# Convolution with residual: weight load as 16 rows on SP's queue, and residual semaphores shared by three

## Chip, cores and metric

The kernel runs on one core of one Trainium2 chip. The metric is the device time of one execution in microseconds (us), taken as the median of several runs. In the profile, times are counted from the start of the span.

## What is computed

A 3 x 3 convolution with zero padding over 16 images of 64 channels and 64 x 64 pixels, to 64 output channels, plus a residual of the same shape as the output; everything is float32 in memory.

```python
def setup_inputs():
    batch, c_in, h, w, c_out, k = 16, 64, 64, 64, 64, 3
    # x: (batch, c_in, h, w), weight: (c_out, c_in, k, k), residual: (batch, c_out, h, w)

x_pad = np.pad(x, ((0, 0), (0, 0), (pad, pad), (pad, pad)), mode='constant')
for b in range(batch):
    for co in range(c_out):
        for ci in range(c_in):
            for kh in range(k):
                for kw in range(k):
                    output[b, co] += weight[co, ci, kh, kw] * x_pad[b, ci, kh:kh+h, kw:kw+w]
return (output + residual).astype(np.float32)
```

## The kernel before

Two images make a pair: 128 partitions (image and channel) of 4096 pixels, 2 MB. There are eight pairs (`NPAIR`), and for each one load of x, one load of the residual and one store of the result. The residual tiles `ro0` to `ro7` all stay in SBUF; DVE adds the convolution into them in place, and they are stored. The raw images go through three buffers `xr` (`NXR`), the packed bfloat16 images through four buffers `xp` (`NXP`), the sums through two halves of PSUM, `ps[0]` and `ps[1]`.

The work of the engines, each with its own hand-written order inside one critical section (L118):

- **SP** issues all large transfers from one queue, in this order: x pair 0 (moved by `to_the_front` ahead of the start barrier), residual 0, x 1, residual 1, x 2, residual 2, then for p = 3 to 7 x p and residual p. Each x load from p = 3 first waits on `s_half` until ACT has read the pair that used the buffer. After the loads come the stores of pairs 0 to 4 (`NEARLY` = 5), each behind a wait `s_add >= 2p + 3`. The stores of pairs 5 to 7 (L77, issued after the section) wait until all engines have finished it.
- **GpSimd** makes a 64 x 64 identity (L133 to L135) and zeroes the borders of `xp` and parts of `wl` (L145 to L148).
- **ACT** issues the weight load `wraw`, 64 rows of 2304 B (L151), on its own queue, and then, for each image, casts the even rows and the odd rows of pixels into the two halves of `xp` (L159, L163).
- **PE** waits for the identity (`s_id`) and the weights (`s_w`), transposes the nine 64 x 64 slices of the weights into PSUM (L195), and then, for each image, runs 24 matmuls (6 weight tiles with 4 chunks of 512 columns; L83 with a weight load, L84 without).
- **DVE** casts the transposed weights into the bfloat16 tile `wl` in six pieces (L172), then adds, for each image, the even and the odd rows of pixels (L182, two instructions). The first of the two raises `s_add`, so `s_add` counts images whose first half is added; the second hands the PSUM half back to PE by `s_bank`.

DVE waits for residual p on a semaphore of its own, `s_r[p]`, once for each pair.

Of the kernel before, what the change touches and what calls it, by code (L numbers as in the profile page):

```python
# [8 lines left out]
FP32 = mybir.dt.float32  # L9
# [6 lines left out]
def kernel(  # L16
# [7 lines left out]
    nc = tc.nc  # L24
# [7 lines left out]
    NPAIR = B // 2  # L32
# [3 lines left out]
    NXR = 3  # L36
# [3 lines left out]
    res_bc = residual.rearrange("b c h w -> (b c) (h w)")  # L40
    out_bc = out.rearrange("b c h w -> (b c) (h w)")
    x_bc = x.rearrange("b c h w -> (b c) (h w)")
    w_flat = weight.rearrange("co ci kh kw -> co (ci kh kw)")

    pool = ctx.enter_context(tc.tile_pool(name="pool", bufs=1))
    psum = ctx.enter_context(tc.tile_pool(name="psum", bufs=1, space=bass.MemoryType.PSUM))

    ident = pool.tile([64, 64], FP32)
    ro = [pool.tile([128, NPIX], FP32, name=f"ro{p}") for p in range(NPAIR)]
    xr = [nc.alloc_sbuf_tensor(f"xr{i}", [128, NPIX], FP32) for i in range(NXR)]  # L50

    xp = [pool.tile([128, J + 1, W], BF16, name=f"xp{i}") for i in range(NXP)]
    wraw = nc.alloc_sbuf_tensor("wraw", [64, 576], FP32)
    wl = pool.tile([128, 2, 3, 2, 64], BF16)
    ps = [psum.tile([128, NCHUNK, JC, W], FP32, name=f"ps{i}") for i in range(2)]

    sem = lambda name: tc.alloc_semaphore(name)
    s_w = sem("s_w")
    s_x = [sem(f"s_x{i}") for i in range(NXR)]
    s_r = [sem(f"s_r{p}") for p in range(NPAIR)]  # L60
    s_out = sem("s_out")
    s_id = sem("s_id")
    s_wt = sem("s_wt")
# [4 lines left out]
    s_add = sem("s_add")  # L68

    def load_x(p):  # L70
        return nc.sync.dma_start(out=xr[p % NXR][:, :], in_=x_bc[128 * p : 128 * p + 128, :]).then_inc(s_x[p % NXR], 16)

    def load_ro(p):
        nc.sync.dma_start(out=ro[p][:, :], in_=res_bc[128 * p : 128 * p + 128, :]).then_inc(s_r[p], 16)

    def store(p):
        return nc.sync.dma_start(out=out_bc[128 * p : 128 * p + 128, :], in_=ro[p][:, :])  # L77

    def matmul(out_, lhsT, rhs, start, stop, ldweights):

        e = nc.tensor
        if ldweights:
            return e.matmul(out=out_, lhsT=lhsT, rhs=rhs, start=start, stop=stop, skip_group_check=True)  # L83
        return e.add_instruction(  # L84
            mybir.InstMatmult(
                name=nc.get_next_instruction_name(),
                engine=PE,
                ins=[e.lower_ap(rhs), e.lower_ap(lhsT)],
                outs=[e.lower_ap(out_)],
                start_tensor_calc=start,  # L90
                stop_tensor_calc=stop,
                tile_size=(128, 128),
                tile_position=(0, 0),
                bass_skip_group_check=True,
                ldweights=False,
            )
        )

    def to_the_front(dma):

        def fixed(ap):
            t = ap.bass_ap.tensor.name
            return mybir.PhysicalAccessPattern(
                ap=ap.ap, offset=ap.bass_ap.offset, dtype=ap.dtype, memref=t, memsetref=t + "_set", bass_ap=ap.bass_ap
            )

        front = nc.main_func.blocks[0].instructions
        here = nc.cur_bb.bb.instructions  # L110
        ins = here.pop()
        assert ins.name == dma.ins.name
        at = next(
            i for i, e in enumerate(front) if e.engine == mybir.EngineType.SP and isinstance(e, mybir.InstDrain)
        )
        front.insert(at, copy.replace(ins, ins=[fixed(a) for a in ins.ins], outs=[fixed(a) for a in ins.outs]))

    with tc.tile_critical(no_gpsimd_drain=True):  # L118

        for p in range(NPAIR):  # L120
            if p >= NXR:

                nc.sync.wait_ge(s_half, 2 * (p - NXR) + 3)
            i = load_x(p)
            if p == 0:
                to_the_front(i)
            load_ro(p)
        for p in range(NEARLY):
            nc.sync.wait_ge(s_add, 2 * p + 3)
            store(p).then_inc(s_out, 16)  # L130


        nc.gpsimd.memset(ident[:, :], 0.0).then_inc(s_id, 1)  # L133
        nc.gpsimd.wait_ge(s_id, 1)
        nc.gpsimd.affine_select(  # L135
            out=ident[:, :],
            in_=ident[:, :],
            compare_op=mybir.AluOpType.not_equal,
            fill=1.0,
            base=0,  # L140
            pattern=[[-1, 64]],
            channel_multiplier=1,
        ).then_inc(s_id, 1)
        for t in xp:
            nc.gpsimd.memset(t[0:64, 0, :], 0.0).then_inc(s_id, 1)  # L145
            nc.gpsimd.memset(t[64:128, J, :], 0.0).then_inc(s_id, 1)  # L146
        nc.gpsimd.memset(wl[0:64, 0, :, 1, :], 0.0).then_inc(s_id, 1)  # L147
        nc.gpsimd.memset(wl[64:128, 1, :, 0, :], 0.0).then_inc(s_id, 1)  # L148


        nc.scalar.dma_start(out=wraw[:, :], in_=w_flat[:, :]).then_inc(s_w, 16)  # L151
        for n in range(B):
            p, im = divmod(n, 2)
            hp = slice(64 * im, 64 * im + 64)
            x4 = xr[p % NXR].rearrange("q (j two w) -> q j two w", two=2, w=W)
            t = xp[n % NXP]
            if im == 0:
                nc.scalar.wait_ge(s_x[p % NXR], 16 * (p // NXR + 1))
            i = nc.scalar.copy(out=t[64:128, 0:J, :], in_=x4[hp, :, 0, :])  # L159
            i.then_inc(s_half, 1)  # L160
            if n >= NXP:
                i._wait_ge(s_conv, n - NXP + 1)
            nc.scalar.copy(out=t[0:64, 1 : J + 1, :], in_=x4[hp, :, 1, :]).then_inc(s_pack, 1)  # L163


        nc.vector.wait_ge(s_wt, 1)
        tpf = ps[0].rearrange("p c j w -> p (c j) w")

        blocks = ((0, 0, 0, 0), (1, 0, 0, 1), (1, 0, 1, 0), (0, 1, 0, 2), (0, 1, 1, 1), (1, 1, 1, 2))
        for half, d, par, kh in blocks:  # L170
            hp = slice(64 * half, 64 * half + 64)
            i = nc.vector.tensor_copy(out=wl[hp, d, :, par, :], in_=tpf[0:64, 3 * kh : 3 * kh + 3, :])  # L172
        i.then_inc(s_bank, 2)
        for n in range(B):
            p, im = divmod(n, 2)
            hp = slice(64 * im, 64 * im + 64)
            o4 = ro[p].rearrange("q (j two w) -> q j two w", two=2, w=W)
            psj = ps[n % 2].rearrange("q c j w -> q (c j) w")
            if im == 0:
                nc.vector.wait_ge(s_r[p], 16)  # L180
            for par in range(2):
                i = nc.vector.tensor_tensor(  # L182
                    out=o4[hp, :, par, :], in0=psj[64 * par : 64 * par + 64, :, :], in1=o4[hp, :, par, :], op=ADD
                )
                if par == 0:
                    i._wait_ge(s_conv, n + 1)

                i.then_inc(s_add if par == 0 or n == B - 1 else s_bank, 1)


        nc.tensor.wait_ge(s_id, 4 + 2 * NXP)
        nc.tensor.wait_ge(s_w, 16)
        wraw3 = wraw.rearrange("p (ci t) -> p ci t", t=9)
        for t in range(9):
            i = nc.tensor.transpose(out=ps[0][0:64, t // 8, t % 8, :], in_=wraw3[:, :, t], identity=ident[:, :])  # L195
        i.then_inc(s_wt, 1)
        with nc.Fori(0, B // NXP, 1, engines=[PE]):
            for n in range(NXP):
                nc.tensor.wait_ge(s_bank, 1).then_inc(s_bank, -1)
                nc.tensor.wait_ge(s_pack, 1).then_inc(s_pack, -1)  # L200
                order = [(1, 0), (1, 1), (0, 0), (0, 1), (2, 0), (2, 1)]
                for i, (kw, d) in enumerate(order):
                    xlo, xhi = max(0, 1 - kw), min(W, W + 1 - kw)
                    for c in range(NCHUNK):
                        j0 = JC * c
                        m = matmul(
                            ps[n % 2][:, c, :, xlo:xhi],
                            wl[:, d, kw, :, :].rearrange("q r c -> q (r c)"),
                            xp[n][:, j0 + d : j0 + d + JC, xlo + kw - 1 : xhi + kw - 1],
                            i == 0,  # L210
                            i == len(order) - 1,
                            c == 0,
                        )
                m.then_inc(s_conv, 1)
# [36 lines left out]
```

## Time and profile before

| | |
|---|---|
| median of 8 runs | 124.32 us (124.07 to 124.86) |
| profiled execution | 124.3 us, span 122.2 us |
| PE, matmuls | 86.7 us busy (71%) |
| DVE | 75.2 us busy (61%) |
| ACT | 62.0 us busy (51%) |
| DMA | 50.48 MB, mean 413 GB/s |
| transposes of the weights, L195 | 9, 1.1 us busy |
| weight casts, L172 | 6, 1.9 us busy |
| weight load, issue to landing | 8.3 us |

The page splits the span into 40 slices of 3.06 us and gives for each the busy tenths of an engine, the mean busy share of the 16 DMA engines and the GB/s they moved. In the list of instructions, a line has start, length, engine, line of the code, operation, output and input, and in brackets the idle time before it with what ended it. In a view by windows, the columns after each engine's busy time are the granted clock of PE, the DMA share and GB/s. PE's clock is given as a share of full speed. "SPq" and "ACTq" are instructions that issue DMAs; q1 is SP's queue of DMA packets and q10 is ACT's.

### The profile page before, as it was taken

What the parts mean: (1) busy time and instruction counts of PE and PEld (TensorE: products, weight loads), DVE (VectorE), ACT (ScalarE), POOL (GpSimd) and SP (SyncE); (2) the same over time, 40 slices, a digit from 0 to 9 for tenths busy, and PEclk for the clock granted to TensorE, in tenths of its full rate; (3) what the DMA queues carried; (4) which work ended last, traced back from release to release, by engine and by line L of the source; (5) the groups of instructions that cost most, each with busy time, mean ns of one, the idle gap of its engine ahead of it and who ended that gap; (6) DMA issues with size and microseconds to landing.
All of it is one profiled execution on the core that took longest, in us unless ns stands there. A gap on an engine that the chain in (4) does not pass through costs nothing.

```text
span 122.2 us, 729 instructions
## 1 busy us (share of the span) xinstructions
PE 86.7 (71%) x389; PEld 10.4 (9%) x105; DVE 75.2 (61%) x38; ACT 62.0 (51%) x33; POOL 2.2 (2%) x16
## 2 busy tenths in 40 slices
PE   0003799999999999999999999999999930000000
PEld 0003000101011110111010101011110100000000
DVE  0005100989889898898989889898898988000000
ACT  4009948966984993992995797599000000000000
POOL 5100000000000000000000000000000000000000
PEclk9999999999999999999999999999999999555555
DMA  6999999999999999999999999999999999999992
GB/s 177 436 331 429 418 429 429 429 429 429 429 429 429 424 434 424 429 429 429 429 429 429 429 429 429 429 429 429 429 434 429 429 429 445 434 434 429 434 434 107
DMA packets 3536, 50.48 MB, mean 413 GB/s; under 512 B 400, under 2 KB 400, under 8 KB 464
## 3 DMA queue, kind: packets, MB, share of 16 engines
q1 hardware_dynamic: 3456, 50.33, 97.7%
q10 hardware_dynamic: 80, 0.15, 0.4%
HBM read 33.70 MB, written 16.78 MB: 413 GB/s over the span
## 4 chain that ended last, share of the span: by engine, by line
PE 70%; DVEq 2%; DVE 2%; issue 0%
PE ps L84 53%; PE ps L83 17%; DVEq L118 2%; DVE ro L182 2%
## 5 line engine op out<-in xcount | busy, mean ns | idle before, releaser
L182 DVE TENSOR_TENSOR ro<-ps,ro 64x2048 f32<-64x2048 f32 x32 | 73.2, 2289 | 17.7 <-PE ps L84 17.2
L84 PE MATMUL ps<-xp,wl 128*128 128x504 bf16 (+1 forms) x288 | 80.0, 388 | 0.2
L159 ACT CAST xp<-xr 64x2048 bf16<-64x2048 f32 x16 | 30.3, 1896 | 21.4 <-DMA xr<-in_x_dram 21.2
L83 PE MATMUL ps<-xp,wl 128*128 128x504 bf16 (+1 forms) x92 | 35.8, 389 | 2.5 <-PEq L200 2.5
L163 ACT CAST xp<-xr 64x2048 bf16<-64x2048 f32 x16 | 30.4, 1897 | 0.4
L83 PEld LDWEIGHTS ps<-xp,wl 128*128 128x128 bf16 x96 | 9.5, 99 | 77.9 <-issue 77.9
L172 DVE CAST wl<-ps 64x192 bf16<-64x192 f32 x6 | 1.9, 347 | 10.6 <-PE ps L195 10.6
L195 PE MATMUL ps<-ident,wraw 64*64 64x64 f32 x9 | 1.1, 309 | 9.4 <-DMA wraw<-in_weight_dram 9.4
L159 ACT ACT_TABLE_LOAD x1 | 1.3, 1283 | 1.5 <-SPq L118 1.5
L195 PEld LDWEIGHTS ps<-ident,wraw 64*64 64x64 f32 x9 | 0.9, 166 | 9.4 <-issue 9.4
L146 POOL MEMSET xp<- 64x64 bf16 x4 | 0.6, 147 | 0.2
L145 POOL MEMSET xp<- 64x64 bf16 x4 | 0.6, 145 | 0.2
L148 POOL MEMSET wl<- 64x192 bf16 x1 | 0.3, 253 | 0.1
L147 POOL MEMSET wl<- 64x192 bf16 x1 | 0.3, 252 | 0.1
L135 POOL TENSOR_SCALAR_AFFINE_SELECT ident<-ident 64x64 f32<-64x64 f32 x1 | 0.2, 233 | 0.2 <-POOL ident L133 0.2
L133 POOL MEMSET ident<- 64x64 f32 x1 | 0.1, 145 | 0.5 <-SPq L118 0.5
L235 POOL MEMSET const-bfloat16-1.0<- 128x1 bf16 x1 | 0.1, 112 | 0.0
L235 POOL MEMSET const-uint8-127<- 128x1 uint8 x1 | 0.1, 112 | 0.0
L235 POOL MEMSET const-float32-1.0<- 128x1 f32 x1 | 0.1, 109 | 0.0
L235 POOL MEMSET const-float32-0.0<- 128x1 f32 x1 | 0.1, 104 | 0.2 <-issue 0.2
## 6 DMA issues: line engine op xcount, KB each, us to landing
xr<-in_x_dram SPq DMA_DIRECT2D x8, 2048.0 KB, 17.6
ro<-in_residual_dram SPq DMA_DIRECT2D x8, 2048.0 KB, 22.1
out_dram<-ro SPq DMA_DIRECT2D x8, 2048.0 KB, 28.7
wraw<-in_weight_dram ACTq DMA_DIRECT2D x1, 144.0 KB, 8.3
```

The lines of the kernel that those rows point to most:

```text
L83: return e.matmul(out=out_, lhsT=lhsT, rhs=rhs, start=start, stop=stop, skip_group_check=True)
L84: return e.add_instruction(mybir.InstMatmult(name=nc.get_next_instruction_name(), engine=PE, ins=[e.lower_ap(rhs), e.lower_ap(lhsT)], outs ...
L118: with tc.tile_critical(no_gpsimd_drain=True):
L145: nc.gpsimd.memset(t[0:64, 0, :], 0.0).then_inc(s_id, 1)
L146: nc.gpsimd.memset(t[64:128, J, :], 0.0).then_inc(s_id, 1)
L147: nc.gpsimd.memset(wl[0:64, 0, :, 1, :], 0.0).then_inc(s_id, 1)
L159: i = nc.scalar.copy(out=t[64:128, 0:J, :], in_=x4[hp, :, 0, :])
L163: nc.scalar.copy(out=t[0:64, 1 : J + 1, :], in_=x4[hp, :, 1, :]).then_inc(s_pack, 1)
L172: i = nc.vector.tensor_copy(out=wl[hp, d, :, par, :], in_=tpf[0:64, 3 * kh : 3 * kh + 3, :])
L182: i = nc.vector.tensor_tensor(out=o4[hp, :, par, :], in0=psj[64 * par : 64 * par + 64, :, :], in1=o4[hp, :, par, :], op=ADD)
L195: i = nc.tensor.transpose(out=ps[0][0:64, t // 8, t % 8, :], in_=wraw3[:, :, t], identity=ident[:, :])
L235: nc = _bacc.Bacc("TRN2", target_bir_lowering=False, num_devices=1)
```

## The change

The weight load leaves ACT. It is issued by SP, behind the first image load and ahead of the first residual load, and it has 16 rows: partition q holds the four output channels 4q to 4q + 3, 9216 B in one piece. A slice for a transpose is now 16 output channels by 64 input channels, so there are 36 transposes in place of 9, each with 64 columns of weights and a 16 x 16 identity as the moving operand; their outputs are written 4 elements apart into the same places of PSUM. The casts into `wl` are the same. The residual loads share three semaphores instead of eight; SP waits, before it issues residual load p for p = 3 to 7, for the first add of image 2(p - 3), and DVE waits for 16, 32 or 48.

```diff
-    ident = pool.tile([64, 64], FP32)
+    ident = pool.tile([16, 16], FP32)
...
-    wraw = nc.alloc_sbuf_tensor("wraw", [64, 576], FP32)
+    wraw = nc.alloc_sbuf_tensor("wraw", [16, 4, 576], FP32)
...
-    s_r = [sem(f"s_r{p}") for p in range(NPAIR)]
+    s_r = [sem(f"s_r{i}") for i in range(NXR)]
...
-        nc.sync.dma_start(out=ro[p][:, :], in_=res_bc[128 * p : 128 * p + 128, :]).then_inc(s_r[p], 16)
+        nc.sync.dma_start(out=ro[p][:, :], in_=res_bc[128 * p : 128 * p + 128, :]).then_inc(s_r[p % NXR], 16)
...
             if p == 0:
                 to_the_front(i)
+                nc.sync.dma_start(out=wraw[:, :, :], in_=w_flat.rearrange("(q u) f -> q u f", u=4)).then_inc(s_w, 16)
+            if p >= NXR:
+
+                nc.sync.wait_ge(s_add, 2 * (p - NXR) + 1)
             load_ro(p)
...
-            pattern=[[-1, 64]],
+            pattern=[[-1, 16]],
...
-        nc.scalar.dma_start(out=wraw[:, :], in_=w_flat[:, :]).then_inc(s_w, 16)
...
-                nc.vector.wait_ge(s_r[p], 16)
+                nc.vector.wait_ge(s_r[p % NXR], 16 * (p // NXR + 1))
...
-        wraw3 = wraw.rearrange("p (ci t) -> p ci t", t=9)
+        wraw4 = wraw.rearrange("q u (ci t) -> q u t ci", t=9)
         for t in range(9):
-            i = nc.tensor.transpose(out=ps[0][0:64, t // 8, t % 8, :], in_=wraw3[:, :, t], identity=ident[:, :])
+            for u in range(4):
+                i = nc.tensor.transpose(
+                    out=ps[0].rearrange("p c j (q u) -> p (c j) u q", u=4)[0:64, t, u, :],
+                    in_=wraw4[:, u, t, :],
+                    identity=ident[:, :],
+                )
         i.then_inc(s_wt, 1)
```

## The prediction

> **What bounds the kernel now.** I read the page's slices first: they show which resource is full.
>
> ```profile
> DVE  0005100989889898898989889898898988000000
> ...
> DMA  6999999999999999999999999999999999999992
> GB/s 177 436 331 429 418 429 429 429 429 429 429 429 429 424 434 424 429 429 429 429 429 429 429 429 429 429 429 429 429 434 429 429 429 445 434 434 429 434 434 107
> ...
> q1 hardware_dynamic: 3456, 50.33, 97.7%
> q10 hardware_dynamic: 80, 0.15, 0.4%
> ```
>
> The DMA engines are full from the first slice to the last. 50.33 MB at 429 GB/s are 117.3 us of a span of 122.2, so the transfers set the time. One slice is low while the engines are fully busy: the third (6.1 to 9.2 us), 331 against 429 GB/s, a loss of 0.23 x 3.06 = 0.70 us. The chain of waits, which ends in PE and DVE, must be read with this: behind it come three stores that the queues would have reached hardly earlier. Next, stages of the start:
>
> ```profile
> 3.00:6.00 3.00, 0.00 (x0) 0.00 (x0) 0.00 (x0) 0.00 (x0) 0.60 (x3) 1.00 1.06 438
> 6.00:9.00 3.00, 0.00 (x0) 0.00 (x0) 0.00 (x0) 0.00 (x0) 0.00 (x0) 1.00 0.95 326
> 9.00:12.00 3.00, 1.14 (x9) 0.93 (x9) 1.39 (x5) 2.86 (x2) 0.00 (x0) 1.00 1.01 431
> ```
>
> The last number is GB/s. The trace's packet records say what runs in the slow stretch: the 64 weight packets of 2304 B (q10) start between 5.09 and 8.34 us, four on each of the 16 engines between its 16 KB packets. From about 6.0 to 8.9 us a 16 KB packet takes 740 to 830 ns; before and after, 611 to 619. Following each engine packet by packet, the excess over 611 ns per large packet is 0.94 to 1.15 us, about 0.97 on all 16: some 0.42 us are the weight packets themselves, some 0.6 the slowed large ones. So 147 KB, worth 0.34 us at full rate, cost 0.97.
>
> Then the start of the compute chain:
>
> ```profile
> 9.12 1.90 ACT L159 CAST xp<-xr 64x2048 bf16<-64x2048 f32 x1 [6.32 <-DMA xr<-in_x_dram]
> ...
> 9.40 1.14 PE L195 MATMUL ps<-ident,wraw 64*64 64x64 f32 x9 [9.40 <-DMA wraw<-in_weight_dram]
> 10.58 1.97 DVE L172 CAST wl<-ps 64x192 bf16<-64x192 f32 x6 [10.58 <-PE ps L195]
> 11.04 1.90 ACT L163 CAST xp<-xr 64x2048 bf16<-64x2048 f32 x1
> ...
> 13.08 0.58 PE L83 MATMUL ps<-xp,wl 128*128 128x512 bf16 x1 [2.54 <-PEq L200]
> ```
>
> The image lands at 9.09 (records of landings), the weights at 9.27. Two branches meet at PE's first convolution, 13.08: ACT's casts end at 12.94, DVE's weight casts at 12.55. The image branch is last; the weight branch has 0.4 us to spare. From there PE runs without a gap (24 matmuls of 216 ns = 5.18 us an image) and DVE follows. The end:
>
> ```profile
> 98.90 4.61 DVE L182 TENSOR_TENSOR ro<-ps,ro 64x2048 f32<-64x2048 f32 x2 [0.58 <-PE ps L84]
> 103.81 1.76 SPq L77 DMA_DIRECT2D out_dram<-ro  x3
> ```
>
> The last three stores are issued from 103.81, 14.6 us of transfer. In the packet records their first packets start at 105.4 to 106.2, directly behind those of the fifth store, with no gap over 6 ns. The first DMA of the kernel, issued at 0.00, had its first packets at 1.01, so these could have started at 104.8. The two engines that land last began at 105.87 and 106.16: the compute chain has a slack of about **1.1 us** against the transfers (1.07 to 1.35). This decides everything below: a gain of the chain is worth nothing, a loss over 1.1 us shows in full.
>
> **What the Trainium skill says.** "DMA: Bandwidth & Descriptors", section "Queues, rings and completion order": each DMA engine takes turns between the queue rows that have work, packet by packet. The trace agrees: weight packets lie singly between large ones. "SBUF — State Buffer", "Door 1: The DMA port swizzle": partitions 0 to 63 reach 8 of 16 ports, 0 to 15 only 4, measured there at 104 GB/s. The trace has no 16-partition load; its 64-partition load does run in a stretch in which everything is 20% slower, which fits. "TensorE: Matmul & The Clock Gate", "LDWEIGHTS": a weight load takes its columns divided by 1.2 GHz, whatever the rows, and may run under the matmul before it; "Part 1" of that page: PE runs at half clock until a free-running window of 3.4 us was busy. The trace agrees with the last: matmuls are 427 ns apart until about 18.5, then 216.
>
> **The change, part by part.**
>
> *Weights on SP's queue.* They leave the second queue, so no packets alternate; on each engine one packet of 9216 B follows the eighth packet of the image and precedes the first residual. It is an issue of 0.33 us (the row of L74) ahead of seven loads on SP; the image load alone keeps the engines in work to about 7 us, so the delay to 1.33 is hidden. ACT loses an issue of 0.53 us while it waits for the image: nothing.
>
> Cost on the stream: at the rate of the large packets 9216/16384 x 611 = 344 ns. Ceiling: if four engines each share one of 4 ports, 147456 B / 104 GB/s = 1.42 us (an estimate with the page's figure). But the end is set by the engine that is last. From the records, without weight packets fifteen engines would finish the image at 6.5 to 7.1 us and the last at 7.59, since its first packet took 2.04 us. It comes to its port when the three others are 0.6 us into theirs: all four finish at about 8.35, a cost of 0.77 for the late one, and the other engines (6.95 + 1.4) are no later than it. So for the end: cost 0.34 to 0.77, against 0.97 now: a gain of 0.2 to 0.63. A loss is not excluded if the ports share badly. I take **-0.4 us**.
>
> *When image and weights land.* The last engine's image packets end at 7.59 instead of 8.34: it lands at about 8.3. The weights follow at 8.6 (no sharing) to 9.0 (ports); I take 8.8 against 9.27.
>
> *36 transposes for 9.* Now 107 ns apart (9 in 1.14 us, the tail included). Each new one has the same 64 columns of weights but 16 moving columns for 64. If the moving side sets the pace, it falls to a quarter, and the load of 64 columns, 53 ns by the page, sets it: 36 x 53 = 1.9 us. If the pace doesn't fall: 36 x 107 = 3.85. In the trace the second weight load ends 59 ns after the first, under the first matmul, so I take 65 ns: 2.3 us. Chain: 8.8 + 0.13 to start + 2.3 + 0.29 tail and signal + 1.97 casts + 0.2 to the matmul = **13.7**, against 13.08. The image branch (8.3 + 3.85) is ready at 12.2, so the weights are now last. PE, DVE and the last stores' issue move by +0.6; the slack of 1.1, less the 0.4 gained by the stream, covers 0.7. On the path: 0, barely. The clock adds noise: PE was at half clock for 5.4 us, and by the page's window it could be 3.4 to 6.8, which moves the chain by -1.0 to +0.7 us.
>
> *Residual semaphores by threes; a wait on s_add ahead of residual loads 3 to 7.* The SP queue stops there: behind it stand the next image load, then stores. Load p waits for the first add of image 2(p-3): 21.1 + 2.3 = 23.4 us for p = 3, then every 10.4 us, to 64.9 for p = 7; today they issue at 21.1 and every 9.8, to 60.4. With +0.6 that is up to 5.1 us later. The next image loads wait until 30.6, 40.4, 50.2 and 60.0 anyway, later than each add (24.0, 34.4, 44.8, 55.1), so none moves. The cover: the queued image load before the last residual lands at 77.6, 12 us after 65.5. Cost 0; were a gap to open, each us would cost one. The stores wait for s_add 3 to 11 as before, the last at 75.7, far ahead of their packets (101). DVE's waits see the same landings.
>
> *Identity 16 x 16*: on GpSimd, done by 3.7 us, under the image load.
>
> **Sum**: the profiled execution took 124.3 (span 122.2 + 2.1 around it), equal to the median 124.32. 124.3 - 0.4 = **123.9 us**. About 0.2% (0.25 us) is what a measurement tells from no change.
>
> **Rivals.**
> - *No gain on the stream.* The 20% stretch is a port or memory limit that stays with the bytes, or isn't the weights' doing: 16 rows into 4 ports cost 0.9 to 1.2 us like now. For: the slowdown begins on all engines at one moment, 6.0, not after each one's own weight packet, which speaks for something shared. Against: the late engine absorbs part. **124.3** (124.1 to 124.5).
> - *The transposes become the bound (slower).* Place: between the weights' landing and the first convolution. At 107 ns each: 8.8 + 0.13 + 3.75 + 0.29 + 1.97 + 0.2 = 15.1, +2.1 us; minus the slack of 1.1: +1.0, hence **125.3**, with an idle gap in the DMA near 104. It decides from +1.1 us, that is from about 80 ns a transpose. For: 107 ns is all that the trace shows for a pair; against: the 59 ns of the second load.
> - *The change doesn't do what it says*, the rows being split or ordered otherwise: as the first rival. The instruction order shows one 16-row load behind the first image, so this is small.
>
> **Chances.** Forecast 0.48 (123.6 to 124.15), no gain 0.29 (the split-row case included), transposes 0.23 (124.5 to 125.4, as the pace lies between). Most of the forecast is below 124.07: faster 0.45, same 0.30, slower 0.25. The range 123.6 to 125.1 leaves out the slowest end of the last and gains over 0.7 us, together under 2 in 10.
>
> **What would show it.** The third slice back above 400 GB/s, weight packets in q1, no 16 KB packet over 700 ns between 6 and 9 us: the stream step right. Weight packets of over 1 us: the ports. The transposes' busy time (about 2.4 us, or near 4) and the start of the first convolution (13.7 or over 14.5) decide the chain; a gap in the GB/s windows at 104 to 107 would show that its slack was used up. Residual loads issued up to 5 us later with no dip in GB/s show the waits free. I am wrong if the third slice recovers and the end doesn't follow, or if the image lands no earlier than 9 us.

## The result and the profile after

The changed kernel takes **125.33 us** (median of 11 runs, 124.57 to 126.09) against 124.28 (32 runs, 124.06 to 124.86) on the same chip: a ratio of 1.008, with a 95% interval of 1.0062 to 1.0098. It is slower by about 1.0 us, outside the predicted range.

The page of the changed kernel, its slices of the span, queues and transposes:

```profile
DVE  0000600689898898989889898898988989100000
...
DMA  7999999999999999999999999999999999999992
GB/s 182 422 272 427 427 427 433 427 433 427 427 427 427 427 427 427 427 427 427 427 427 433 427 427 427 433 427 433 427 433 427 427 427 443 433 427 433 427 449 117
...
q1 hardware_dynamic: 3488, 50.48, 98.2%
...
L199 PE MATMUL ps<-ident,wraw 16*64 16x16 f32 x36 | 2.3, 213 | 9.9 <-DMA wraw<-in_weight_dram 9.9
```

The weights are in q1 now, as intended, and the third slice has become worse: 272 GB/s where it was 331 and should have been over 400. The windows of the same trace (columns as before: busy times, clock, DMA share, GB/s):

```profile
3.00:6.00 3.00, 0.00 (x0) 0.00 (x0) 0.00 (x0) 0.00 (x0) 0.51 (x3) 1.00 1.00 426
6.00:9.00 3.00, 0.00 (x0) 0.00 (x0) 0.00 (x0) 0.11 (x1) 0.00 (x0) 1.00 1.05 279
9.00:12.00 3.00, 2.08 (x36) 2.11 (x36) 0.00 (x0) 2.98 (x2) 0.00 (x0) 1.00 0.94 399
```

From 6 to 9 us the DMA engines are fully busy (1.05) although the rate is low: the packets take longer, the engines don't wait. In the packet records, the 16 weight packets of 9216 B take 347 to 1099 ns, two of them over 1 us, and 17 of the 16 KB packets beside and behind them take 970 to 1570 ns, where 611 is usual. Weight packets and slowed large packets together come to 1.56 us an engine (1.03 in the kernel before, counted the same way). No engine is spared: the first of the 16 to land residual 0 does so at 13.42 us, 12.81 before. The start of the compute chain and its end, from the timeline:

```profile
8.89 1.90 ACT L162 CAST xp<-xr 64x2048 bf16<-64x2048 f32 x1 [6.65 <-DMA xr<-in_x_dram]
...
9.92 2.27 PE L199 MATMUL ps<-ident,wraw 16*64 16x16 f32 x36 [9.92 <-DMA wraw<-in_weight_dram]
...
12.22 1.97 DVE L175 CAST wl<-ps 64x192 bf16<-64x192 f32 x6 [12.22 <-PE ps L199]
...
14.49 0.58 PE L83 MATMUL ps<-xp,wl 128*128 128x512 bf16 x1 [2.30 <-PEq L208]
...
105.14 1.76 SPq L77 DMA_DIRECT2D out_dram<-ro  x3
```

The first convolution starts at 14.49 (13.08 before), the last stores are issued at 105.14 (103.81), 1.33 us later. But the windows from 103 to 112 us show no dip: 426, 431 and 426 GB/s. In the packet records these stores start at 106.16 at the earliest. Five engines have finished the store ahead by then and wait up to 0.4 us; the last one finishes it at 106.88 and goes on without a gap, so the end is not moved by this. The last landing is at 121.80 (121.28).

The span of this execution is 122.73 us, its time 125.94: **3.2 us lie outside the span**, where the kernel before has 2.1 (2.05 to 2.15 in all its executions whose spans are on record). Over 13 executions of the changed kernel, spans are 122.3 to 123.5 (mean 122.78; 122.09 in those executions of the kernel before), the time outside 2.03 to 3.29 (mean 2.47). So the loss has two parts: +0.7 in the span and +0.4 outside it. The prediction had no cause for the second at all.

### The profile page after: what moved, and what is told of

The parts are those of the page before. It is cut to its first block, busy times and chain, and to the rows that moved or that the text cites. A ratio compares the mean times of both kernels' runs of the same rounds, so it can differ in the third digit from the quotient of the medians.

```text
span 122.7 us, 779 instructions
## 1 busy us (share of the span) xinstructions
PE 87.6 (71%) x412; PEld 11.7 (10%) x132; DVE 75.2 (61%) x38; ACT 62.0 (50%) x33; POOL 2.1 (2%) x16
## 4 chain that ended last, share of the span: by engine, by line
PE 70%; DVEq 2%; DVE 2%; issue 0%
PE ps L84 53%; PE ps L83 17%; DVEq L118 2%; DVE ro L185 2%
## 5 line engine op out<-in xcount | busy, mean ns | idle before, releaser
L199 PE MATMUL ps<-ident,wraw 16*64 16x16 f32 x36 | 2.3, 213 | 9.9 <-DMA wraw<-in_weight_dram 9.9
L199 PEld LDWEIGHTS ps<-ident,wraw 16*64 16x64 f32 x36 | 2.2, 149 | 9.9 <-issue 9.9
```

The lines of the kernel that those rows point to most:

```text
L199: i = nc.tensor.transpose(out=ps[0].rearrange("p c j (q u) -> p (c j) u q", u=4)[0:64, t, u, :], in_=wraw4[:, u, t, :], identity=ident[:, :],)
```

## The experiments

Ratios are to the kernel before on the same chip, with 95% intervals. To compare streams, I take from the trace when residual 0, the first transfer behind the weights, lands: the mean over its 16 DMA engines (before 13.34 us, changed kernel 13.90).

**The place in the queue alone.** The 64 rows of before, moved to SP's queue behind the first image:

```diff
                 to_the_front(i)
+                nc.sync.dma_start(out=wraw[:, :], in_=w_flat[:, :]).then_inc(s_w, 16)
...
-        nc.scalar.dma_start(out=wraw[:, :], in_=w_flat[:, :]).then_inc(s_w, 16)
```

> The kernel before, with its 64 weight rows of 2304 B moved to SP's queue behind the first image load (nothing else changed). Theory (ports: the 16 rows share 4 SBUF ports, so each engine pays 1.5 us for them): 64 rows reach 8 ports, so the stall is about half, 0.7 us an engine against 0.97 of before; weights land near 9.0, chain unmoved; 124.0 to 124.2. Rival A (the place in SP's queue is what hurts, since an engine can't pass a slow weight packet): as slow as the change, 125.0 to 125.4. Rival B (only the transposes matter): 124.2 to 124.3.

Measured: 124.11 us, ratio 0.9998 (0.9991 to 1.0006). The third slice rises to 382 GB/s, residual 0 lands at 13.15, the first convolution starts at 12.14. The move does no harm, and hardly any good.

**The 16 rows alone**, on ACT's queue, with the 36 transposes and eight residual semaphores:

```diff
-        nc.scalar.dma_start(out=wraw[:, :], in_=w_flat[:, :]).then_inc(s_w, 16)
+        nc.scalar.dma_start(out=wraw[:, :, :], in_=w_flat.rearrange("(q u) f -> q u f", u=4)).then_inc(s_w, 16)
...
```

> 16 rows of 9216 B and 36 transposes, but issued on ACT's own queue, with the residual semaphores of before. Theory (ports): the same stall as in the change, large packets of over 1 us near the weight packets, last landing +0.5 us, chain +1.0 to +1.4: 124.9 to 125.4. Rival A (place in SP's queue): no stall on the stream; only the 36 transposes, chain +1.3: 124.5. Rival B (transposes alone): as the change, 125.3, with a stream like before.

Measured: 125.86 us, 1.0118 (1.0099 to 1.0136); third slice 278 GB/s, residual 0 at 14.22, time outside the span 2.50 to 2.94. That is slower than expected. Both parts of the loss are here without the queue being touched: they come with the 16 rows and what is built on them.

**The residual semaphores and SP's waits alone** (the diff's lines on `s_r` and `s_add`, nothing else):

> The kernel before with the residual semaphores by threes and the waits on s_add only. Theory and both rivals: 124.3, residual loads issued 3 to 5 us later and no change in GB/s. If the waits cost: over 124.6.

Measured: 124.16 us, 0.9999 (0.9988 to 1.0009). And the change without this part (16 rows on SP, eight semaphores, no wait on `s_add`):

> The change without its residual part: own semaphores for each pair, no waits on s_add ahead of residual loads. All theories: as the change, 125.0 to 125.5, span 122.3 to 123.3, with time minus span over 2.3 in some runs (PE's program is as long as in the change). Under 124.6 would say that the waits are part of the loss.

Measured: 125.38 us, 1.0089 (1.0056 to 1.0121), as slow as the whole change. The waits cost nothing in either direction.

**More transposes** in the kernel before, three small ones ahead of each of the nine:

```diff
         for t in range(9):
+            for u in range(3):
+                nc.tensor.transpose(out=ps[1][0:64, t // 8, t % 8, 16 * u : 16 * u + 16], in_=wraw3[0:16, :, t], identity=ident[0:16, 0:16])
```

> The kernel before with 27 more small transposes (16 rows, 64 columns of weights, 16 moving columns) whose output is not used; weight load as before. They add 27 x 59 ns = 1.6 us, of which 0.4 is spare: chain +1.2, stream as before. Theory (slack of 1.1 us at the end): 124.3 to 124.7, with more spread than before. Rival B (transposes are the whole loss): 125.2 or more.

Measured: 125.73 us, 1.011 (1.009 to 1.013). The 36 took 4.9 us, not the 2.3 of the changed kernel: 16-row transposes in a row start 59 ns apart, but a 64-row one starts 145 ns after a 16-row one, and a 16-row one 247 ns after a 64-row one. As a copy of the change's PE work this run failed. It measures something else well. Its last stores are issued at 107.67, 3.86 us later than before, and its windows show what the changed kernel's don't:

```profile
102.00:104.00 2.00, 0.73 (x4) 0.00 (x0) 1.42 (x2) 0.00 (x0) 0.00 (x0) 1.00 1.01 434
104.00:107.00 3.00, 0.00 (x0) 0.00 (x0) 2.97 (x2) 0.00 (x0) 0.00 (x0) 1.00 0.54 229
107.00:108.50 1.50, 0.00 (x0) 0.00 (x0) 0.38 (x1) 0.00 (x0) 0.00 (x0) 0.80 0.03 11
108.50:111.00 2.50, 0.00 (x0) 0.00 (x0) 0.00 (x0) 0.00 (x0) 0.00 (x0) 0.50 0.99 413
```

The transfers run dry (11 GB/s) until the stores come. This execution took 126.81 against 124.30, so 3.86 us of delay cost 2.51: the slack of the chain is about 1.3 us. The 1.33 of the changed kernel fit in, all the more as its stream is 0.5 us late itself.

**The load's form alone.** The 16 rows go behind the first image into a tile of their own, and the nine transposes work on a constant tile, so that PE's program is that of before. This version and the next three leave the weights out of the result.

```diff
+    wd = nc.alloc_sbuf_tensor("wd", [16, 2304], FP32)
...
+                nc.sync.dma_start(out=wd[:, :], in_=w_flat.rearrange("(q u) f -> q (u f)", u=4)).then_inc(s_w, 16)
...
+        nc.gpsimd.memset(wraw[:, :], 0.1).then_inc(s_id, 1)
...
-        nc.scalar.dma_start(out=wraw[:, :], in_=w_flat[:, :]).then_inc(s_w, 16)
```

> The 16-row load on SP's queue behind the first image load into a tile of its own, with PE's nine transposes of before reading a constant 64-row tile once that load has landed: the weights are left out of the computation, every instruction of the conv stays. So the load alone, without the 27 more transposes. Theory (ports): stall of 1.5 us an engine as in the change, weights landing near 9.8, first conv near 13.5, last landing +0.5 us, span 122.6, time minus span 2.07: 124.7. Rival B (transposes): 124.2.

Measured: 124.57 us, 1.0039 (1.0027 to 1.0051), 2.10 to 2.15 outside the span. The load's form costs 0.48 us, all inside the span. The same bytes as 128 rows of 1152 B, over all partitions:

> As the run before it, but the load is one of 128 rows of 1152 B over all 128 partitions (weights left out of the computation again). Theory (ports): each engine writes to a port of its own, no large packet over 640 ns, excess about 0.4 us an engine, image landing near 8.0: 123.8 to 124.1. If the stall comes from small packets or from the weights' place in memory: excess 0.7 or more, above the 64 rows of before.

Measured: 123.13 us, **0.9926** (0.9912 to 0.9941). The line of the window from 6 to 9 us, for the 16 rows and for the 128:

```profile
6.00:9.00 3.00, 0.00 (x0) 0.00 (x0) 0.00 (x0) 0.50 (x1) 0.00 (x0) 1.00 1.01 289
```

```profile
6.00:9.00 3.00, 0.77 (x8) 0.80 (x9) 0.00 (x0) 1.25 (x1) 0.00 (x0) 1.00 0.99 415
```

289 against 415 GB/s for the same bytes in the same place of the same queue. With 128 rows no large packet takes over 611 ns between 5.5 and 10 us. It is faster than expected: residual 0 lands 0.75 us earlier than before, and at the end the last engine is 0.3 us behind the median instead of 0.6. Is it the number of rows or that of the partitions' ports? 32 rows in partitions 0 to 31:

> The same with 32 rows of 4608 B in partitions 0 to 31, two packets an engine, eight ports (weights left out of the computation again). Theory (ports): as the 64 rows on SP's queue, excess about 0.7 us an engine, since the ports are the same eight: 124.0 to 124.2. If the size or number of packets decides: between 0.8 and 1.5 us.

Measured: 124.27 us, 1.0006 (0.9991 to 1.0022), third slice 354. And the 16 rows of 9216 B again, now in every eighth partition, which changes nothing but the partitions:

```diff
-    wd = nc.alloc_sbuf_tensor("wd", [16, 2304], FP32)
+    wd = nc.alloc_sbuf_tensor("wd", [128, 2304], FP32)
...
-                nc.sync.dma_start(out=wd[:, :], in_=w_flat.rearrange("(q u) f -> q (u f)", u=4)).then_inc(s_w, 16)
+                nc.sync.dma_start(out=wd[0:128:8, :], in_=w_flat.rearrange("(q u) f -> q (u f)", u=4)).then_inc(s_w, 16)
```

> The run with 16 rows of 9216 B and nine transposes on a constant tile (weights left out of the computation) again, with one thing changed: the rows lie in every eighth partition of 128, which reach 8 ports and not 4. Theory (ports): excess 0.7 to 0.9 us an engine against 1.3, last landing 0.4 us earlier, 124.1 to 124.3. If the size of the packets or their number decides: 124.6 and excess 1.3 as with adjacent rows.

Measured: 124.19 us, 0.9996 (0.9986 to 1.0006). The line of the window that had 289 GB/s above:

```profile
6.00:9.00 3.00, 0.00 (x0) 0.00 (x0) 0.00 (x0) 0.57 (x1) 0.00 (x0) 1.00 0.96 333
```

16 packets of 9216 B spread over the partitions cost what 32 or 64 smaller ones cost in the first 32 or 64, and 0.5 us less, by the ratios, than the same 16 in partitions 0 to 15. It is where the rows lie that counts. The Trainium skill ("SBUF — State Buffer", "Door 1: The DMA port swizzle") counts 4 ports for partitions 0 to 15, 8 for 0 to 31, for 0 to 63 and, by its formula, for every eighth, and 16 for all. It doesn't say what such a load does to other transfers. The runs fall into these three classes, and two pairs of them differ in the partitions alone as far as the load goes (the first and third row, the fourth and fifth):

| load of the weights | ports by the page | residual 0 lands | ratio |
|---|---|---|---|
| 16 rows in 0 to 15 | 4 | 13.72 | 1.0039 |
| 32 rows in 0 to 31 | 8 | 13.26 | 1.0006 |
| 16 rows in every eighth | 8 | 13.32 | 0.9996 |
| 64 rows in 0 to 63, SP's queue | 8 | 13.15 | 0.9998 |
| 64 rows in every second | 16 | 12.67 | 0.9944 |
| 128 rows | 16 | 12.59 | 0.9926 |

**A version that is faster.** The fifth row of the table computes everything: 64 rows of 2304 B in every second partition of a zeroed tile of 128, on SP's queue behind the first image, and nine transposes with a 128 x 128 permutation that brings the odd rows, all zero, out of the way.

```diff
-    wraw = nc.alloc_sbuf_tensor("wraw", [64, 576], FP32)
+    wraw = nc.alloc_sbuf_tensor("wraw", [128, 576], FP32)
...
+                nc.sync.wait_ge(s_z, 1)
+                nc.sync.dma_start(out=wraw[0:128:2, :], in_=w_flat[:, :]).then_inc(s_w, 16)
...
+        nc.gpsimd.memset(wraw[:, :], 0.0).then_inc(s_z, 1)
...
-            i = nc.tensor.transpose(out=ps[0][0:64, t // 8, t % 8, :], in_=wraw3[:, :, t], identity=ident[:, :])
+            i = nc.tensor.transpose(out=tpw[0:64, 128 * t : 128 * t + 128], in_=wraw3[:, :, t], identity=ident[:, :])
```

> A version meant to keep what the ports give: the kernel before, with its 64 rows of 2304 B on SP's queue behind the first image load, but in every second partition of 128, so that they reach 16 ports; GpSimd zeroes the tile first, SP waits for that, and the nine transposes take 128 rows and a 128 x 128 permutation. PE's program is as long as before. Theory (ports): excess about 0.45 us an engine, image landing near 7.9, weights near 8.2, transposes 9 x 213 ns, first conv near 12.5, last landing near 120.2: 123.2 to 123.5. If the ports are not the cause: as the 64 contiguous rows on SP's queue, 124.1.

Measured: 123.5 us, **0.9944** (0.9928 to 0.9960): faster than both kernels. Its page shows the third slice repaired:

```profile
GB/s 167 426 421 432 432 432 432 432 426 426 432 421 432 426 432 432 432 432 432 432 426 432 432 421 432 426 426 426 432 432 432 432 432 432 432 432 432 432 432 130
```

**The time outside the span.** In the traces of the changed kernel, of the 16 rows on ACT's queue and of the change without its residual part, the packet records hold one packet of 16 KB of a queue q8, kind "instruction", 1.7 to 2.4 us after the last instruction; the kernel before has none. In these three the packet ends 3.43, 3.17 and 2.80 us after the last instruction, and the time outside the span is 3.21, 2.93 and 2.58 us: 0.2 us less each time, so the one goes with the other. What these three share is PE's program, 54 instructions longer (27 more transposes, a weight load and a matmul each). So: the kernel before, with 27 transposes of the identity ahead of PE's wait for the weights, done while the image loads.

```diff
+        for t in range(27):
+            nc.tensor.transpose(out=ps[1][0:64, t // 8, t % 8, :], in_=ident[:, :], identity=ident[:, :])
         nc.tensor.wait_ge(s_w, 16)
```

> The kernel before with 27 transposes of the identity (54 more PE instructions, as many as the change adds) put ahead of PE's wait for the weights, where PE idles under the image load; their output is not used. Weight load, stream and chain as before. Theory T3 (in the change, PE's longer program costs 0.4 to 1.2 us outside the span in some runs, since more instructions have to be fetched): span 122.1 as before, time minus span above 2.1 in some runs, median 124.3 to 125.2. Rival (that time comes from something else in the change): time minus span 2.07 in every run, 124.2.

Measured: 124.55 us, 1.0036 (1.0016 to 1.0055), and not evenly: of 22 executions, 10 are like before (spans to 122.3, 2.0 outside), 5 have 2.46 to 3.58 outside, 7 have spans of 122.7 to 123.2. With nine such transposes in place of 27:

> As the run with 27 hidden transposes, with 9 of them (18 more PE instructions instead of 54). If the length of PE's program makes the time outside the span: fewer runs over 2.3 us, or none, median 124.1 to 124.3. If any hidden PE work does: as many as with 27 (5 of 22).

Measured: 124.10 us, 0.9992 (0.9983 to 1.0002); all as before. So hidden PE work that nobody waits for costs nothing in 18 instructions and 0.45 us in 54. The length of the program could be the cause, or PE's work at the start, by moving its clock. To part them, the same 27 transposes behind PE's last matmul, where it is idle:

```diff
                 m.then_inc(s_conv, 1)
+        nc.tensor.wait_ge(s_bank, 1)
+        for t in range(27):
+            nc.tensor.transpose(out=ps[0][0:64, (t % 32) // 8, t % 8, :], in_=ident[:, :], identity=ident[:, :])
```

> The kernel before with 27 more 64 x 64 transposes of the identity (54 PE instructions[...]), placed behind PE's last matmul, where PE waits only for image 14 to be added and is done some 3 us before DVE; nothing waits for them. Theory (length of PE's program, fetched as instructions): as the kernel with the same 54 instructions at the start: mean +0.3 to +0.5 us, a part of the executions with 2.4 to 3.6 us outside the span in place of 2.1. Rival (the instructions' work at the start moves PE's clock): equal to the kernel before, within 0.15%, all executions at 2.1 outside the span.

Measured: 125.08 us, 1.0069 (1.0053 to 1.0084), at 2.0 to 2.12 outside the span in all 6 executions; the loss is all inside. The clock is excluded, as nothing at the start differs. That it would show outside the span, as I had expected, was wrong. Its timeline at the end and its page's queues:

```profile
98.09 1.53 PEld L217 LDWEIGHTS ps<-ident 64*64 64x64 f32 x27 [1.08 <-DVE ro L182]
98.09 1.69 PE L217 MATMUL ps<-ident 64*64 64x64 f32 x27
98.20 4.61 DVE L182 TENSOR_TENSOR ro<-ps,ro 64x2048 f32<-64x2048 f32 x2 [0.58 <-PE ps L84]
103.10 1.61 SPq L77 DMA_DIRECT2D out_dram<-ro  x3
```

```profile
q1 hardware_dynamic: 3456, 50.33, 97.1%
q10 hardware_dynamic: 80, 0.15, 0.4%
q8 instruction: 1, 0.02, 0.0%
```

The transposes end at 99.8, three us before DVE, and the stores are issued even earlier than before: no engine is late. But q8 is on the page, with one packet. It ran from 101.42 us for 0.97 us, in the middle of the stores. How far the last of the 16 engines lands behind their median, transfer by transfer:

```
transfer landing at (us)     86.8   91.6   96.4  101.3  106.2  111.0  115.9  120.7
before                       0.62   0.60   0.61   0.60   0.60   0.61   0.59   0.61
27 at the end                0.24   0.23   0.26   0.38   1.36   1.39   1.33   1.31
```

From the transfer after the packet on, one engine lands 1 us later than the last one did until then, and stays so to the end, since all have equal work and none has a pause. The records carry no number of the engine, but the lags of the fifteen others stay as they were and one near 0 is gone, so it lost about 1.4 us: the fetch itself, and 0.4 on the 16 KB packet that starts as the fetch ends, which takes 1005 ns in place of 611. The last store lands at 122.01 (121.28). In the run with more transposes the same packet came at 38.5 us, and its last engine goes from 0.31 to 1.41 behind the median there, until the gap at 105 wipes it out. So **one 16 KB fetch of instructions costs its DMA engine 1 us for itself and some 0.4 on the packet beside it, and where the DMA sets the end, as here, the kernel is 0.9 us later** (125.08 against 124.16).

The same work in a loop of one transpose was to show it from the other side:

> The kernel before with the same 27 transposes of the identity ahead of PE's wait for the weights, but written as a loop of one transpose, so that PE's program grows by a few instructions only. Theory (length of the program): equal to the kernel before, within 0.15%, and 2.1 us outside the span in every execution. Rival (work at the start moves the clock): +0.3 to +0.4% with spans of 122.7 to 123.2 us in a third of the executions.

Measured: 127.0 us, 1.0204 (1.018 to 1.0227). Both theories missed: a turn of the loop takes 382 to 428 ns, where the same transposes in a row start 107 ns apart, so that the transposes ran past the weights' landing and the stores were issued at 107.85. That is 4.04 us late, and with the slack of 1.3 it explains 2.7 of the 2.8 us. There is no q8 packet and 2.02 to 2.12 outside the span; beyond that it tells nothing. Last, 60 transposes at the end:

> As the version with 27 transposes behind the last matmul, but with 60 (120 PE instructions, [...]3.6 us of PE's idle time at the end, of which about 4.5 us are there). Theory (length): at least as slow as with 27, +0.3 to +1.0 us, more executions with a long time outside the span, or all. Rival: equal to the kernel before, unless the transposes end after DVE (then up to +0.2 us).

Measured: 125.14 us, 1.0078 (1.0062 to 1.0093), again one fetch, at 102.58 us: hardly more than with 27. The cost goes by the fetch, not by the instruction. (The profiled execution, 125.55 us, is the slowest of the six; one engine is 1.2 us behind the median there before the fetch, and why the trace doesn't show.)

## Why the prediction was wrong, point by point

- *The cost on the stream, "0.34 to 0.77 for the end", since "the late engine absorbs part":* **this step failed.** It let the four engines that meet at a port delay one another only, with slower engines finding room. The records show every engine slowed, and the large packets behind the weights too: residual 0 lands 0.56 us later than before in the mean of all engines, instead of 0.4 earlier, and the last engine of all moves as far as the median does (121.28 to 121.80, 120.7 to 121.2). The 16 rows alone, with nothing else of the change, cost 0.48 us. The 4 ports were the right mechanism: the ceiling of 1.42 us an engine, which I worked out and then argued down, is about what came (1.35 in the version with nine transposes, 1.56 in the changed kernel, weight packets and slowed large ones together), and so did the sign named for it, weight packets of over 1 us. The first rival, "no gain on the stream", was nearest, though it priced the rows too low, at 0.9 to 1.2 us: the slowdown at one moment on all engines, "something shared", was the evidence to follow.
- *Excess of before, 0.97 us:* right as a reading (the slowed packets begin at 5.6 us and range from 0.65 to 0.95, wider than I read), wrong in what would cure it. It was not the second queue (moving the 64 rows to SP gave -0.02%), but that partitions 0 to 63 reach 8 ports: over 16 ports hardly any large packet is slowed.
- *Landing of image and weights:* 8.87 and 9.78 measured, 8.3 and 8.8 predicted; follows from the first. (In the mean of the 16 engines the image lands 0.45 us earlier than before, at 7.86; its last engine gains only half of that.)
- *Transposes at 65 ns, 2.3 us:* right; they are 59 ns apart. The slower rival, the transposes as the bound, ended at about the measured time (125.3), but by luck: its mechanism did not happen, the transposes were fast and the end did not wait for them.
- *First convolution at 13.7:* it was 14.49, 0.79 later. The weights' landing alone was 0.98 later; the other terms came out 0.19 shorter. *Slack of 1.1:* somewhat more. The two engines that land last finish the store ahead at 106.16 and 106.34 (I had read 105.87 and 106.16), 1.3 to 1.5 us after 104.8, and the run with more transposes gives 1.3. It held.
- *Waits on `s_add`, cost 0:* right. SP's issues in the changed kernel, image and residual in turn:

```profile
21.29 0.33 SPq L71 DMA_DIRECT2D xr<-in_x_dram  x1
24.74 0.33 SPq L74 DMA_DIRECT2D ro<-in_residual_dram  x1
31.14 0.33 SPq L71 DMA_DIRECT2D xr<-in_x_dram  x1
35.12 0.33 SPq L74 DMA_DIRECT2D ro<-in_residual_dram  x1
```

  The residual loads go out 3.6 to 5.9 us later than before, and the image loads keep their pace. No slice of the page after the third is under 427 GB/s, but for the last, and the run with this part alone is as fast as before.
- *Time outside the span, 2.1 unchanged:* **the second failure, an omission.** I priced 36 transposes for 9 by their time on PE, and not the 54 instructions as bytes to be fetched. The Trainium skill has it ("Runtime: NRT & Kernel Launch", "Instruction fetch mechanics"): instructions come in blocks of 16 KB by a DMA of the sequencer's own, "mostly hidden". The size agrees; that it is hidden does not, where the DMA engines are the bound.

Together: 0.48 (load's form) and 0.45 (longer program, as measured at the start of PE's work) make 0.93 of the 1.0 us. The second term is the less certain: the same instructions at the end of PE's work cost 0.9. **What stays open:** when the fetch comes. It fell behind the last instruction in three traces, in mid-run in three; 10 of the 22 executions with 27 early transposes show no cost, and the profiled one has no such packet. I take the changed kernel's executions with 2.35 to 3.29 us outside the span for fetches behind it, and part of those with spans of 122.8 to 123.5 for fetches inside, but only one of its executions has a trace, and it shows the first kind. Nor is it known at what length a program begins to need the block; it lies between 18 and 54 instructions more than before.

## What to carry to other kernels

In a kernel that the DMA bounds, judge a small load by where its partitions lie, not by its packet size or its queue alone: spread it over all 128 partitions, by stride if need be, even at the price of small packets. And count instructions as traffic: unrolled work that is free on its engine can bring one more block of instructions, and one such fetch cost this kernel 0.9 us; it need not fall where the added code stands.

## What the runs showed that was not expected

- 128 packets of 1152 B beat 16 of 9216 B by 1.2% of the whole kernel (123.13 against 124.57 us). The Trainium skill ("DMA: Bandwidth & Descriptors", "Rules for kernel authors") says that it is not measured which is faster, 16 large descriptors or 128 small ones over all partitions. Its 16 fill a tile of one partition and these 16 lay in 16 partitions, so the runs settle it only for this case.
- A delay of one DMA engine is not made up while the stream is full: the lag of 1.3 to 1.4 us in the run with 27 transposes at the end stays the same within 0.1 us over four transfers, and that in the run with more transposes from the fetch at 38.5 us until the gap at 105.
- Transposes of 64 rows and of 16 rows in turn cost 0.53 us for a group of three small ones and a large one, against 0.28 us at the pace of equal ones in a row (59 and 107 ns).
